# Twelve seven-product steps instead of nine, with one of the three sums on GpSimd and a single ring for the split weights

## The chip, the cores and the metric

One core of a Trainium2 chip runs the whole kernel. The metric is the device time of one execution in microseconds (us). Engines are called TensorE (PE in the profile, PEld for its weight loads), VectorE (DVE), ScalarE (ACT), GpSimd (POOL) and SyncE (SP); SP and POOL issue the DMA transfers.

## The reference

A decoder trunk with `DEPTH = 1`, so only layer 0 and the final norm are computed:

```python
def reference(x, norm_attn, w_in_attn, w_out_attn, ..., final_norm):
    h = x                                     # (1, 256, 4096) float32
    h = h + attn_branch(rms_norm(h, norm_attn), w_in_attn, w_out_attn)
    return rms_norm(h, final_norm)

def attn_branch(xn, w_in, w_out):             # w_in (4096, 16384), w_out (4096, 4096)
    q, k, v, g = jnp.split(xn @ w_in, 4, axis=-1)
    o = stick_breaking_attention(to_heads(q), to_heads(k), to_heads(v))   # 32 heads of 128
    return (o * jax.nn.silu(g)) @ w_out
```

Nearly all the work is the two matrix products, 256 rows of x against 256 MB and 64 MB of float32 weights.

## The kernel before, in words

**Precision.** TensorE multiplies a reduced float32 (fp32r). Each operand is therefore split in two: a high part, a cast on ACT (`wh`), and a low part, the difference on DVE (`wl`, called a low here). One product is three matmuls of 128 x 512: high by high, high by low, low by high (`mm3`).

**Units and steps.** The output is made in units. Units 0 to 15 go over column blocks of the input weights (two column tiles of 512 each: q and k, gate and v), units 16 to 18 over pairs of column blocks of the output weights, and two single units end the kernel. Each unit has 16 steps over the 4096 inner rows; a step takes two weight tiles (`raw`, 128 x 2 x 512, float32), one for each column tile, each with two inner blocks. Seen as a 2 x 2 matrix of blocks by a 2 x 2 matrix of blocks, a step costs eight products in the plain way. In a mixed unit (1 to 15, 17 and 18) the steps of the list `SEVEN` use a Strassen form with seven products, at the price of sums of weight blocks. The other steps have eight products and no sums of weights.

**A seven-step.** The first raw tile is split as it came (part i = 0, two blocks, forms A11 and A12). Of the second tile the second block is split as it came (part 1, form S4). A transfer issued by POOL then adds that second block from memory onto the tile's first block (`add_block`, two DMAs with `accum_op=ALU.add`). Then come three sums of blocks (`sums`), all on DVE: `one[0] -= two[0]`, `two[1] = one[0] + two[1]`, `one[1] += one[0]`. The four summed blocks are split as two parts of two blocks each (i = 2 and 3).

**Rings.** Raw tiles live in 7 places, filled by SP in the order of the steps. The split pairs live in 5 places (`w`), the split single blocks in 2 (`s`). A ring's place is set free when the last product that uses the part is done.

**What sets the order.** The kernel is written as small generators. A planner (`Plan`) runs them in simulated time: each work has an engine, a cost and a key (a due time), and whenever an engine is free in that simulated time the waiting work with the least key is emitted. The result is one fixed instruction order for each engine; the semaphores are put in afterwards. So costs such as `vector_ns`, keys such as `first[c] - SUMS_AHEAD * 1e3` and the order of the list `parts` decide the order, and nothing else of them is left at run time.

Of the kernel before, what the change touches and what calls it, by code (L numbers as in the profile page):

```python
# [11 lines left out]
F32R = mybir.dt.float32r  # L12
BF16 = mybir.dt.bfloat16
AF = mybir.ActivationFunctionType
ALU = mybir.AluOpType
# [4 lines left out]
P = 128  # L20
# [8 lines left out]
W = 2 * CW  # L29
NJ = D // W  # L30
KT = 2
NS = KC // KT
# [6 lines left out]

SEVEN = (1,3,5,7,8,10,11,13,14)
RAW_BUFS = 7
PAIRS = 5
SINGLES = 2
KEPT = PAIRS

SPREAD = (11, 1.1)
HEADS_AHEAD = 3
HEADS_LATER = 12  # L50
AHEAD, SUMS_AHEAD = 4.0, 3.0
PIPE = 0
BLOCKS_LATER = 2


# [7 lines left out]

BOTH, SECOND = slice(0, 2), slice(1, 2)
SEVEN_PARTS = (
    (0, BOTH, ((1, "A11", 0), (2, "A12", 1))),
    (1, SECOND, ((3, "S4", 0),)),
    (1, BOTH, ((7, "S3", 0), (5, "S1", 1))),  # L70
    (0, BOTH, ((6, "S2", 0), (4, "A22", 1))),
)
EIGHT_PARTS = (
    (0, BOTH, ((2, "A11", 0), (2, "A12", 1), (4, "A21", 0), (4, "A22", 1))),
# [12 lines left out]

def scalar_ns(n):
    return 98 + n / 1.2


def tensor_ns(n):
# [138 lines left out]
def kernel(  # L231
# [10 lines left out]
    nc = Plan(tc)  # L242
# [3 lines left out]
    wp = ctx.enter_context(tc.tile_pool(name="weights", bufs=1))  # L246
# [25 lines left out]
    parts, quads = [], []  # L272
    for u, (kind, w, cols) in enumerate(units):
        for s in range(NS):
            if kind == "single":
                if s % 2 == 0:
                    quads.append(((w, cols[0], s), (w, cols[0], s + 1)))
                b = ((1, 6), (7, 2))[u - LAST + 1]
# [10 lines left out]
            for i, (k, place, prods) in enumerate(which):  # L289
                parts.append(  # L290
                    dict(u=u, s=s, i=i, tile=(len(quads) - 1, k), place=place, prods=prods, quad=len(quads) - 1,
                         seven=which is SEVEN_PARTS, size=place.stop - place.start)
                )

    if PIPE:
        late, turn = [], []
        for k, p in enumerate(parts):
            if p["seven"] and p["i"] > 1 and p["s"] < NS - 1:
                late.append(p)
                continue  # L300
            turn.append(p)
            if late and p["s"] != late[0]["s"] and (p["i"] == 1 if p["seven"] else p["i"] == 0):
                now = [q for q in late if q["s"] < p["s"] or q["u"] < p["u"]]
                turn += now
                late = [q for q in late if q not in now]
        assert not late and len(turn) == len(parts)
        parts = turn
# [6 lines left out]
    starts, ends, first, left, place_of = {}, {}, {}, {}, {}  # L314
    PRODUCT = 3 * tensor_ns(W)
    for g, (n, k) in enumerate(order):
        p = parts[n]
        b = p["u"], p["prods"][k][0]
# [19 lines left out]
    def dve(emit, n, key=None, **kw):  # L338
        n = n if isinstance(n, tuple) else (n,)
        cost = sum(vector_ns(m) for m in n) + 122 * (len(n) - 1)  # L340
        return nc.work("vector", cost, emit, soon() if key is None else key, **kw)

    def act(emit, n, key=None, **kw):
        n = n if isinstance(n, tuple) else (n,)
        cost = sum(scalar_ns(m) for m in n) + 100 * (len(n) - 1)
        return nc.work("scalar", cost, emit, soon() if key is None else key, **kw)
# [5 lines left out]
        return nc.work("tensor", 90 + sum(tensor_ns(m) for m in n), emit, nc.here - 1e4, wait=400)  # L352

    def moved(engine, emit, sizes, key, after=None, hold=False, adds=False):
        issue = 550 if engine == "gpsimd" else 330
        return nc.work(
            engine, issue * len(sizes), emit, key, after=after, hold=hold, moves=[(4 * P * n, adds) for n in sizes]
        )

    def together(*works):  # L360
        for w in works:
            nc.start(w)

    for name, places in (
        ("raw", RAW_BUFS), ("w", PAIRS), ("s", SINGLES), ("gh", 3), ("one", 1), ("two", 1),
        ("qkh", 1), ("qkl", 1), ("f", 1), ("att", 1), ("heads", 1),
        *((f"b{b}", 1) for b in range(1, 8)),
    ):
        nc.ring(name, places)


    raw, wh, wl = {}, {}, {}
    lows_left, tile_left = {}, {}
    quad_parts = {}
# [38 lines left out]
    def tile_done(*tile):  # L413
        tile_left[tile] -= 1
        if not tile_left[tile]:
            nc.give("raw")
# [6 lines left out]

    def sums(q):

        a, b, c, d = quad_parts[q]
        one, two = raw[q, 0], raw[q, 1]
        for k in range(2):
            tile_left[q, k] += 1

        def add(to, at_, f, g, key, op=ALU.add):
            return dve(
                lambda: nc.vector.tensor_tensor(out=to[:, :, at_, :], in0=f, in1=g, op=op), W,
                key - SUMS_AHEAD * 1e3,
            )

        yield nc.until(("lows", a), ("T3", q))
        yield add(one, 0, one[:, :, 0, :], two[:, :, 0, :], first[c], ALU.subtract)
        yield nc.until(("lows", b))
        yield add(two, 1, one[:, :, 0, :], two[:, :, 1, :], first[c])  # L440
        nc.tell(("sums", c))
        yield add(one, 1, one[:, :, 0, :], one[:, :, 1, :], first[d])
        nc.tell(("sums", d))
        for k in range(2):
            tile_done(q, k)

    def piece(n, c, there):

# [9 lines left out]
            nc.tell(("low", n, k))  # L458
        low_done(n)

    def split(size, tag, bufs):
        for n, p in enumerate(parts):
            if p["size"] != size:
                continue
            q = p["quad"]
            yield nc.take(tag)
            t = p["tile"][1]
            if q:
                yield nc.until(("raw", q, t))
            wh[n] = wp.tile([P, size, W], F32R, tag=tag + "h", name=f"wh{n}", bufs=bufs)  # L470
            wl[n] = wp.tile([P, size, W], F32R, tag=tag + "l", name=f"wl{n}", bufs=bufs)
            cuts = [slice(k, k + 1) for k in range(KT)] if q == 0 else [slice(0, size)]
            lows_left[n] = len(cuts)
            if p["seven"] and p["i"] == 0:
                nc.start(sums(q))
            for c in cuts:
                if q == 0:
                    there = [("raw", q, t, c.start)]
                else:
                    there = [("sums", n)] if p["seven"] and p["i"] > 1 else [("raw", q, t)]  # L480
                nc.start(piece(n, c, there))


# [105 lines left out]
    for _ in range(WARM):  # L589
# [8 lines left out]
        out=bound, in_=bound, compare_op=ALU.is_gt, fill=0.0, base=0,  # L598
# [23 lines left out]
    def x_stats():  # L622
        for i in range(NT * NQ):
            t, q = divmod(i, NQ)
            w = D // NQ
            yield nc.until(("used", 0, 1 + i * 11 // 16))
            yield nc.take("gh")
            nc.start(x_stat(i, t, q, w))
# [41 lines left out]
    def constants():  # L670
        yield nc.until(("form", "s", 0))
        yield dve(lambda: nc.vector.tensor_copy(neg_tri, tri_f), P)
        nc.give("qkl")
# [293 lines left out]

    def new_h(c):

        if c == NJ - 2:  # L970
            both = wp.tile([P, HG, KT, CW], F32, tag="raw", name=f"h{c}", bufs=RAW_BUFS)
        for t in range(NT):
            if c == NJ - 2:
                hs[c, t] = both[:, t].rearrange("p k n -> p (k n)")
                continue
            pool, tag, bufs = (ep, f"h{c}_{t}", 1)
            if NJ - 4 <= c < NJ - 2:
                pool, tag, bufs = wp, "s" + "hl"[t], SINGLES
            elif c == NJ - 1:
                pool, tag = sp, "x" + "hl"[t] + "0"  # L980
            hs[c, t] = pool.tile([P, W], F32, tag=tag, name=f"h{c}_{t}", bufs=bufs)

# [80 lines left out]
    def mixed_h(u, c):  # L1063
        yield nc.until(("full", u, 1))
        if c + 1 == NJ - 3:
            yield nc.take("s", "s")
        for k in range(2):
            new_h(c + k)
        yield from combine(u, Rows(c), Rows(c + 1), ("C1", "C2"))
        yield nc.until(("C1", u), ("C2", u))  # L1070
        nc.tell(("C", u))
# [61 lines left out]
    def count_down(*name):  # L1133
        left[name] -= 1
        return not left[name]

    def done(n, k):
        p = parts[n]
        u, s = p["u"], p["s"]
        if ends[u, p["prods"][k][0]] == (n, k):  # L1140
            nc.tell(("full", u, p["prods"][k][0]))
        if count_down("part", n):
            nc.give("w" if p["size"] == KT else "s")
        if count_down("step", u, s):
            nc.tell(("used", u, s))

# [12 lines left out]
    def products():  # L1159
        for g, (n, k) in enumerate(order):  # L1160
            p = parts[n]
            u, s = p["u"], p["s"]
            b, f, c = p["prods"][k]
            if u < 1:
                what = "s"
            elif u < OUT0:
                what = "n"
            elif u == OUT0:
                what = "o"
            else:  # L1170
                what = "r" if u > LAST - 2 and s in SEVEN else "p"
            if starts[u, b] == (n, k):
                yield nc.take(f"b{b}")
                ev.setdefault(u, {})[b] = acc.tile([P, W], F32, tag=f"b{b}", name=f"acc{u}_{b}")
            yield nc.until(("low", n, c), ("form", what, s), lead=nc.LEAD)
            yield nc.work(
                "tensor", PRODUCT, lambda: product(n, k), g * PRODUCT, after=lambda n=n, k=k: done(n, k), hold=False
            )
            nc.here = g * PRODUCT

    together(split(KT, "w", PAIRS), split(1, "s", SINGLES), products(), x_stats(), x_factor(), constants())

    def in_turn(works):
        for w in works:
# [54 lines left out]
```

## Time and profile before

| | |
|---|---|
| median of 3 runs | 1756.4 us (1754.83 to 1757.13) |
| profiled execution, its span | 1754.0 us |
| busy in that span: PE, PEld, DVE, ACT, POOL | 1736.9, 1427.1, 1560.4, 1166.4, 295.7 us |
| mean granted TensorE clock | 0.997 |
| bytes moved by DMA | 405.86 MB, mean 231 GB/s |

The page gives no other time of the profiled execution than its span, so the span stands for it. A busy time is the union of an engine's instructions; all helpers record under one line (L115), so groups are told apart by tile names: `wh` casts, `wl` lows, `raw` sums and loads, `acc` products, `f`, `a`, `z`, `o` the heads' work between units.

### The profile page before, as it was taken

What the parts mean: (1) busy time and instruction counts of PE and PEld (TensorE: products, weight loads), DVE (VectorE), ACT (ScalarE), POOL (GpSimd) and SP (SyncE); (2) the same over time, 40 slices, a digit from 0 to 9 for tenths busy, and PEclk for the clock granted to TensorE, in tenths of its full rate; (3) what the DMA queues carried; (4) which work ended last, traced back from release to release, by engine and by line L of the source; (5) the groups of instructions that cost most, each with busy time, mean ns of one, the idle gap of its engine ahead of it and who ended that gap; (6) DMA issues with size and microseconds to landing.
All of it is one profiled execution on the core that took longest, in us unless ns stands there. A gap on an engine that the chain in (4) does not pass through costs nothing.

```text
span 1754.0 us, 24699 instructions
## 1 busy us (share of the span) xinstructions
PE 1736.9 (99%) x7806; PEld 1427.1 (81%) x7806; DVE 1560.4 (89%) x1971; ACT 1166.4 (67%) x1594; POOL 295.7 (17%) x364
## 2 busy tenths in 40 slices
PE   8999999999999999999999999999999999999997
PEld 6888888888888888888888888888888888888885
DVE  7889999999999999999999999999999997899963
ACT  7975767676767676767676767676767675666543
POOL 0012121111111121211111111111112111111100
PEclk9999999999999999999999999999999999999998
DMA  9968777777777878787878787878786877889874
GB/s 340 316 192 224 230 218 229 223 223 226 222 228 217 239 210 239 208 245 210 240 208 245 208 239 206 242 202 245 200 246 200 262 244 239 229 245 271 257 236 156
DMA packets 242867, 405.86 MB, mean 231 GB/s; under 512 B 27520, under 2 KB 67968, under 8 KB 242736
## 3 DMA queue, kind: packets, MB, share of 16 engines
q1 hardware_dynamic: 193968, 352.15, 60.8%
q0 software_dynamic: 47184, 49.76, 17.3%
q10 hardware_dynamic: 1584, 2.38, 0.4%
q8 instruction: 61, 1.00, 0.2%
q14 instruction: 70, 0.57, 0.1%
HBM read 396.05 MB, written 8.13 MB: 230 GB/s over the span
## 4 chain that ended last, share of the span: by engine, by line
PE 92%; DVE 3%; issue 2%; DMA 2%; ACT 1%; SPq 0%; ACTq 0%; DVEq 0%
PE acc L115 87%; PE z L115 2%; DVE wl L115 2%; PE o L115 2%; DMA raw<-in_w_in_dram 1%; PE tr L115 1%; ACT wh L115 1%; DVE raw L115 0%; ACT h L115 0%; SPq L115 0%; DMA xres<-in_x_dram 0%; DMA raw<-in_w_out_dram 0%; ACTq L115 0%; DVE gv_sb L115 0%; DVE h L115 0%
## 5 line engine op out<-in xcount | busy, mean ns | idle before, releaser
L115 ACT CAST wh<-raw 128x1024 fp32r<-128x1024 f32 (+1 forms) x948 | 886.1, 976 | 476.1 <-issue 173.3
L115 DVE TENSOR_TENSOR wl<-raw,wh 128x1024 fp32r<-128x1024 f32 (+1 forms) x948 | 1032.1, 1131 | 125.3 <-ACT wh L115 118.6
L115 PE MATMUL acc<-wh,sh 128*128 128x512 f32 x1913 | 762.6, 399 | 2.4 <-DVE sh L115 2.1
L115 PE MATMUL acc<-wh,sl 128*128 128x512 f32 x1913 | 746.2, 390 | 0.0
L115 PE MATMUL acc<-wl,sh 128*128 128x512 f32 x1913 | 744.9, 389 | 0.8 <-DVE wl L115 0.8
L115 PEld LDWEIGHTS acc<-wh,sh 128*128 128x128 f32 x1913 | 359.4, 188 | 77.3 <-DVE gv_sb L115 3.9
L115 PEld LDWEIGHTS acc<-wh,sl 128*128 128x128 f32 x1913 | 359.1, 188 | 76.9 <-DVE sl L115 0.8
L115 PEld LDWEIGHTS acc<-wl,sh 128*128 128x128 f32 x1913 | 359.7, 188 | 71.5 <-DVE wl L115 1.5
L115 POOL DMA_DIRECT2D raw<-in_w_in_dram x270 | 236.1, 987 | 1075.7 <-DMA raw<-in_w_in_dram 403.1
L115 DVE TENSOR_TENSOR raw<-raw,raw 128x512 f32<-128x512 f32 x306 | 210.3, 687 | 5.1
L115 PE MATMUL acc<-wh,oh 128*128 128x512 f32 x494 | 193.2, 391 | 0.0
L115 PE MATMUL acc<-wl,oh 128*128 128x512 f32 x494 | 192.4, 389 | 0.6 <-DVE wl L115 0.6
L115 PE MATMUL acc<-wh,ol 128*128 128x512 f32 x494 | 192.3, 389 | 0.0
L115 PEld LDWEIGHTS acc<-wl,oh 128*128 128x128 f32 x494 | 92.8, 188 | 20.5 <-DVE wl L115 1.2
L115 PEld LDWEIGHTS acc<-wh,oh 128*128 128x128 f32 x494 | 92.8, 188 | 19.3 <-DVE gv_sb L115 0.4
L115 PEld LDWEIGHTS acc<-wh,ol 128*128 128x128 f32 x494 | 92.7, 188 | 19.2
L115 DVE TENSOR_TENSOR raw<-raw 128x512 f32<-128x512 f32 x153 | 104.5, 683 | 0.0
L115 POOL DMA_DIRECT2D raw<-in_w_out_dram x36 | 31.6, 992 | 132.5 <-DMA raw<-in_w_out_dram 66.2
L115 ACT ACTIVATE f<-f 128x384 f32<-128x384 f32 x96 | 50.5, 526 | 3.0
L115 DVE SCALAR_TENSOR_TENSOR f<-z,f 128x384 f32<-128x384 f32 x32 | 17.8, 557 | 31.2 <-ACT f L115 31.2
L115 POOL DMA_DIRECT2D p<-spill x33 | 20.3, 696 | 129.6 <-DVE ol L115 94.0
L115 ACT ACTIVATE gl<-gl 128x512 f32<-128x512 f32 x48 | 30.0, 625 | 7.3 <-DVE gl L115 7.3
(90 smaller groups left out, 745.9 us busy)
## 6 DMA issues: line engine op xcount, KB each, us to landing
raw<-in_w_in_dram SPq DMA_DIRECT2D x1020, 256.0 KB, 4.6
raw<-in_w_out_dram SPq DMA_DIRECT2D x256, 256.0 KB, 3.9
raw<-in_w_in_dram POOLq DMA_DIRECT2D x270, 128.0 KB, 5.2
raw<-in_w_out_dram POOLq DMA_DIRECT2D x36, 128.0 KB, 5.6
xr<-in_x_dram SPq DMA_DIRECT2D x16, 256.0 KB, 5.2
xres<-in_x_dram SPq DMA_DIRECT2D x16, 256.0 KB, 5.6
xs<-in_xT_dram SPq DMA_DIRECT2D x15, 256.0 KB, 5.3
spill<-gated POOLq DMA_DIRECT2D x15, 256.0 KB, 3.9
```

The lines of the kernel that those rows point to most:

```text
L115: return self.tc.keep_in_program_order(getattr(self.engine, name)(*args, **kw))
```

## The change

1. `SEVEN` has twelve steps instead of nine.
2. The third sum is an add on GpSimd, started after the first sum and due 25 us (`POOL_AHEAD`) ahead of its product in the planner's terms. The planner's cost for a GpSimd transfer rises from 550 to 950 ns.
3. The four summed blocks are four parts of one block each (i = 2 to 5). For steps below 14 the last two (i = 4 and 5) stand behind the first two parts of the next step in the list `parts`.
4. All split blocks share one tile of twelve places, freed block by block; a pair takes two neighbouring places, with a skip at the ring's end.
5. Near the end, the output tiles that lay in the ring `s` lie in two more places of the raw ring.

```diff
-SEVEN = (1,3,5,7,8,10,11,13,14)
+SEVEN = (1, 2, 3, 5, 6, 7, 9, 10, 11, 12, 13, 14)
 RAW_BUFS = 7
-PAIRS = 5
-SINGLES = 2
-KEPT = PAIRS
+SLOTS = 12
+KEPT = 5
-PIPE = 0
+PIPE = 1
+LATE_UNTIL = 14
+LATE_FROM = 4
+POOL_AHEAD = 2.5e4
 SEVEN_PARTS = (
     (0, BOTH, ((1, "A11", 0), (2, "A12", 1))),
     (1, SECOND, ((3, "S4", 0),)),
-    (1, BOTH, ((7, "S3", 0), (5, "S1", 1))),
-    (0, BOTH, ((6, "S2", 0), (4, "A22", 1))),
+    (1, FIRST, ((7, "S3", 0),)),
+    (0, FIRST, ((6, "S2", 0),)),
+    (1, SECOND, ((5, "S1", 0),)),
+    (0, SECOND, ((4, "A22", 0),)),
 )
+def pool_ns(n):
+    return 400 + 2.9 * n
...
-            if p["seven"] and p["i"] > 1 and p["s"] < NS - 1:
+            if p["seven"] and p["i"] >= LATE_FROM and p["s"] < LATE_UNTIL:
...
-        issue = 550 if engine == "gpsimd" else 330
+        issue = 950 if engine == "gpsimd" else 330
...
+        def last():
+            yield pool_add(one[:, :, 1, :], one[:, :, 0, :], one[:, :, 1, :], first[e] - POOL_AHEAD)
+            nc.tell(("sums", e))
+            tile_done(q, 0)
+
         yield nc.until(("lows", a), ("T3", q))
         yield add(one, 0, one[:, :, 0, :], two[:, :, 0, :], first[c], ALU.subtract)
+        nc.tell(("sums", c))
+        nc.start(last())
         yield nc.until(("lows", b))
-        yield add(two, 1, one[:, :, 0, :], two[:, :, 1, :], first[c])
-        nc.tell(("sums", c))
-        yield add(one, 1, one[:, :, 0, :], one[:, :, 1, :], first[d])
+        yield add(two, 1, one[:, :, 0, :], two[:, :, 1, :], first[d])
         nc.tell(("sums", d))
...
+    hi_ring = wp.tile([P, SLOTS, W], F32R, name="wh")
+    lo_ring = wp.tile([P, SLOTS, W], F32R, name="wl")
...
-            yield nc.take(tag)
+            if at_ + size > SLOTS:
+                extra = SLOTS - at_
+                at_ = 0
+            yield nc.take(*["w"] * (size + extra))
...
-        if c == NJ - 2:
+        if NJ - 4 <= c < NJ - 1:
             both = wp.tile([P, HG, KT, CW], F32, tag="raw", name=f"h{c}", bufs=RAW_BUFS)
...
-        if count_down("part", n):
-            nc.give("w" if p["size"] == KT else "s")
+        place_uses[n, c] -= 1
+        if not place_uses[n, c]:
+            nc.give(*["w"] * slots_of[n][c])
```

How the order changes on DVE, in the middle of a mixed unit of the attention part. Before, one seven-step: `raw_0_7118` is its first raw tile, `raw_1_7071` its second.

```order
L115 TENSOR_TENSOR wl_7202<-raw_0_7118,wh_7201 128x1024
L115 TENSOR_TENSOR raw_0_7118<-raw_0_7118,raw_1_7071 128x2x256
L115 TENSOR_TENSOR raw_1_7071<-raw_0_7118,raw_1_7071 128x2x256
L115 TENSOR_TENSOR raw_0_7118<-raw_0_7118 128x2x256
L115 TENSOR_TENSOR wl_7225<-raw_1_7071,wh_7224 128x1024
L115 TENSOR_TENSOR wl_7235<-raw_0_7118,wh_7234 128x1024
L115 TENSOR_TENSOR wl_7252<-raw_0_7131,wh_7251 128x1024
```

Now, in such a unit: `raw_0_6791` and `raw_1_6783` are the two tiles of one seven-step, 6776 and 6751 those of the step before, 6855 and 6802 those of the step after. The low of its own first pair stands a few rows ahead of this piece.

```order
L123 TENSOR_TENSOR raw_0_6791<-raw_0_6791,raw_1_6783 128x2x256
L123 TENSOR_TENSOR wl<-raw_1_6751,wh 128x512
L123 TENSOR_TENSOR wl<-raw_0_6776,wh 128x512
L123 TENSOR_TENSOR wl<-raw_0_6855,wh 128x1024
L123 TENSOR_TENSOR wl<-raw_1_6802,wh 128x512
L123 TENSOR_TENSOR wl<-raw_1_6783,wh 128x512
L123 TENSOR_TENSOR raw_1_6783<-raw_0_6791,raw_1_6783 128x2x256
L123 TENSOR_TENSOR wl<-raw_0_6791,wh 128x512
L123 TENSOR_TENSOR raw_0_6855<-raw_0_6855,raw_1_6802 128x2x256
L123 TENSOR_TENSOR wl<-raw_1_6783,wh 128x512
L123 TENSOR_TENSOR wl<-raw_0_6791,wh 128x512
```

The three sums in a row have become two that stand apart, with the lows of the neighbouring steps between; the lows of pairs of summed blocks are single ones, and the last two of a step stand behind the next step's first sum.

On POOL, in the attention part. Before, only transfers (the added blocks, and one spill of a unit's gated heads):

```order
L115 DMA raw_1_8577<-in_w_in_dram 128x256 x2
L115 DMA spill_8688<-gated_8506 128x512
L115 DMA raw_1_8673<-in_w_in_dram 128x256 x2
L115 DMA raw_1_8746<-in_w_in_dram 128x256 x2
L115 DMA raw_1_8817<-in_w_in_dram 128x256 x2
```

Now:

```order
L123 DMA raw_1_8403<-in_w_in_dram 128x256 x2
L123 TENSOR_TENSOR raw_0_8395<-raw_0_8395 128x2x256
L123 DMA raw_1_8454<-in_w_in_dram 128x256 x2
L123 TENSOR_TENSOR raw_0_8446<-raw_0_8446 128x2x256
L123 TENSOR_TENSOR raw_0_8493<-raw_0_8493 128x2x256
L123 DMA raw_1_8582<-in_w_in_dram 128x256 x2
```

An add stands between most pairs of transfers, so a transfer can be queued behind an add and an add behind a transfer. On TensorE the list of matmul rows is 153 shorter (7561 to 7408), which is 51 products of three.

More of the change, by code (lines that the diff above doesn't have):

```diff
@@ L62 @@
 PLACES = {f: k for forms in (SEVEN_FORMS, EIGHT_FORMS) for k, f in enumerate(forms)}
-BOTH, SECOND = slice(0, 2), slice(1, 2)
+BOTH, FIRST, SECOND = slice(0, 2), slice(0, 1), slice(1, 2)
 SEVEN_PARTS = (
@@ L341, in dve, with pool_add @@
         return nc.work("vector", cost, emit, soon() if key is None else key, **kw)
+    def pool_add(to, f, g, key, op=ALU.add):
+        return nc.work(
+            "gpsimd", pool_ns(W), lambda: nc.gpsimd.tensor_tensor(out=to, in0=f, in1=g, op=op), key
+        )
     def act(emit, n, key=None, **kw):
@@ L364 @@
     for name, places in (
-        ("raw", RAW_BUFS), ("w", PAIRS), ("s", SINGLES), ("gh", 3), ("one", 1), ("two", 1),
+        ("raw", RAW_BUFS), ("w", SLOTS), ("gh", 3), ("one", 1), ("two", 1),
         ("qkh", 1), ("qkl", 1), ("f", 1), ("att", 1), ("heads", 1),
@@ L424, in sums @@
     def sums(q):
-        a, b, c, d = quad_parts[q]
+        a, b, third, c, d, e = quad_parts[q]
         one, two = raw[q, 0], raw[q, 1]
@@ L435, in add @@
             )
+        def last():
+            yield pool_add(one[:, :, 1, :], one[:, :, 0, :], one[:, :, 1, :], first[e] - POOL_AHEAD)
+            nc.tell(("sums", e))
+            tile_done(q, 0)
         yield nc.until(("lows", a), ("T3", q))
         yield add(one, 0, one[:, :, 0, :], two[:, :, 0, :], first[c], ALU.subtract)
+        nc.tell(("sums", c))
+        nc.start(last())
         yield nc.until(("lows", b))
-        yield add(two, 1, one[:, :, 0, :], two[:, :, 1, :], first[c])
-        nc.tell(("sums", c))
-        yield add(one, 1, one[:, :, 0, :], one[:, :, 1, :], first[d])
+        yield add(two, 1, one[:, :, 0, :], two[:, :, 1, :], first[d])
         nc.tell(("sums", d))
-        for k in range(2):
-            tile_done(q, k)
+        tile_done(q, 1)
     def piece(n, c, there):
@@ L459, in piece, with split @@
         low_done(n)
-    def split(size, tag, bufs):
-        for n, p in enumerate(parts):
-            if p["size"] != size:
-                continue
-            q = p["quad"]
-            yield nc.take(tag)
+    hi_ring = wp.tile([P, SLOTS, W], F32R, name="wh")
+    lo_ring = wp.tile([P, SLOTS, W], F32R, name="wl")
+    place_uses, slots_of = {}, {}
+    for n, p in enumerate(parts):
+        for _, _, c in p["prods"]:
+            place_uses[n, c] = place_uses.get((n, c), 0) + 1
+    def split():
+        at_ = 0
+        for n, p in enumerate(parts):
+            size, q = p["size"], p["quad"]
+            extra = 0
+            if at_ + size > SLOTS:
+                extra = SLOTS - at_
+                at_ = 0
+            yield nc.take(*["w"] * (size + extra))
+            slots_of[n] = [1] * size
+            slots_of[n][0] += extra
             t = p["tile"][1]
@@ L469, in split @@
                 yield nc.until(("raw", q, t))
-            wh[n] = wp.tile([P, size, W], F32R, tag=tag + "h", name=f"wh{n}", bufs=bufs)
-            wl[n] = wp.tile([P, size, W], F32R, tag=tag + "l", name=f"wl{n}", bufs=bufs)
+            wh[n] = hi_ring[:, at_ : at_ + size, :]
+            wl[n] = lo_ring[:, at_ : at_ + size, :]
+            at_ += size
             cuts = [slice(k, k + 1) for k in range(KT)] if q == 0 else [slice(0, size)]
@@ L479, in split @@
                 else:
-                    there = [("sums", n)] if p["seven"] and p["i"] > 1 else [("raw", q, t)]
+                    there = [("raw", q, t)]
+                    if p["seven"] and p["i"] > 1:
+                        there = [("T3", q) if p["i"] == 2 else ("sums", n)]
                 nc.start(piece(n, c, there))
@@ L968, in new_h @@
     def new_h(c):
-        if c == NJ - 2:
+        if NJ - 4 <= c < NJ - 1:
             both = wp.tile([P, HG, KT, CW], F32, tag="raw", name=f"h{c}", bufs=RAW_BUFS)
         for t in range(NT):
-            if c == NJ - 2:
+            if NJ - 4 <= c < NJ - 1:
                 hs[c, t] = both[:, t].rearrange("p k n -> p (k n)")
@@ L976, in new_h @@
             pool, tag, bufs = (ep, f"h{c}_{t}", 1)
-            if NJ - 4 <= c < NJ - 2:
-                pool, tag, bufs = wp, "s" + "hl"[t], SINGLES
-            elif c == NJ - 1:
+            if c == NJ - 1:
                 pool, tag = sp, "x" + "hl"[t] + "0"
@@ L1065, in mixed_h @@
         if c + 1 == NJ - 3:
-            yield nc.take("s", "s")
+            yield nc.take("raw", "raw")
         for k in range(2):
@@ L1141, in done @@
             nc.tell(("full", u, p["prods"][k][0]))
-        if count_down("part", n):
-            nc.give("w" if p["size"] == KT else "s")
+        c = p["prods"][k][2]
+        place_uses[n, c] -= 1
+        if not place_uses[n, c]:
+            nc.give(*["w"] * slots_of[n][c])
         if count_down("step", u, s):
@@ L1179, in products @@
             nc.here = g * PRODUCT
-    together(split(KT, "w", PAIRS), split(1, "s", SINGLES), products(), x_stats(), x_factor(), constants())
+    together(split(), products(), x_stats(), x_factor(), constants())
     def in_turn(works):
```

## The prediction

> **What bounds the kernel now.** I read the page's busy times first, then the chain that ended last, then the chain in order of time, then a table of stretches.
>
> ```profile
> span 1754.0 us, 24699 instructions
> PE 1736.9 (99%) x7806; PEld 1427.1 (81%) x7806; DVE 1560.4 (89%) x1971; ACT 1166.4 (67%) x1594; POOL 295.7 (17%) x364
> PE 92%; DVE 3%; issue 2%; DMA 2%; ACT 1%; SPq 0%; ACTq 0%; DVEq 0%
> 222.85 48.33 PE acc L115 x213
> 396.56 48.31 PE acc L115 x213
> 1440.66 157.10 PE acc L115 x693
> 560.00:650.00 90.00, 90.00 (x410) 74.10 (x409) 82.53 (x100) 61.98 (x83) 16.29 (x19) 1.00 0.80 225
> 650.00:740.00 90.00, 90.00 (x409) 74.16 (x408) 82.89 (x101) 59.87 (x80) 16.33 (x19) 1.00 0.78 228
> ```
>
> TensorE makes 92% of the chain. The columns of the stretches are length, busy PE, PEld, DVE, ACT, POOL, then granted clock, DMA share and GB/s: in the middle PE is busy 90.00 of 90.00 us at clock 1.00. A piece of the chain that recurs, 48.3 us of 213 matmuls, starts at 222.85 and again at 396.56: two units of the program in 173.71 us, so **86.86 us a unit**. 693 matmuls in 157.10 us are 0.2267 us each, so a product of three matmuls takes **0.680 us**. DVE stands close behind: (82.53 + 82.89) / 180 = 91.9% of the time, 79.8 us of each unit. ACT (60.9 of 90) and POOL (16.3 of 90) are far off.
>
> The span of the profiled execution is 1754.0 us, 2.4 below the median of the runs, 1756.4; I make the sum as a difference and put it on the median. Runs lie within 1754.83 to 1757.13, so about 0.2% (3.5 us) is what a measurement can tell from no change.
>
> **What goes from TensorE.** A step of a mixed unit with eight products becomes one with seven in three more of the sixteen steps. There are 15 mixed units on the input weights and 2 on the output weights: 17 x 3 = 51 products, 51 x 0.680 = **34.7 us** off the engine that sets the end. If all else kept up, a unit would take 86.86 - 2.04 = 84.82 us and the kernel 1756.4 - 34.7 = **1721.7 us**. This is the floor of the range.
>
> **What comes to DVE.** Rates first. DVE instructions overlap at their ends, so the interval from start to start counts.
>
> ```profile
> 757.62 3.50 DVE L115 TENSOR_TENSOR wl<-raw,wh 128x1024 fp32r<-128x1024 f32 x3 [0.64 <-ACT wh L115]
> 785.82 0.68 DVE L115 TENSOR_TENSOR gv_sb<-acc,gv_sb 128x512 f32<-128x512 f32 x1
> 786.42 1.21 DVE L115 TENSOR_TENSOR wl<-raw,wh 128x1024 fp32r<-128x1024 f32 x1
> 787.55 0.68 DVE L115 TENSOR_TENSOR gv_sb<-acc,gv_sb 128x512 f32<-128x512 f32 x1
> ```
>
> An add of 512 columns lets the next one start after 0.60 us (785.82 to 786.42), one of 1024 after 1.13 us (786.42 to 787.55), each 0.08 us before its own end. A seven-step had three lows of 1024, one of 512 and three sums: 3 x 1.13 + 4 x 0.60 = 5.79 us. Now it has one low of 1024, five of 512 and two sums: 1.13 + 7 x 0.60 = 5.33. So the cut into single blocks costs 4 x 0.60 - 2 x 1.13 = 0.14 and the sum that leaves saves 0.60. An eight-step keeps two lows, 2.26. Per unit: 9 x 5.79 + 7 x 2.26 = 67.9 before, 12 x 5.33 + 4 x 2.26 = 73.0 after, **+5.1 us**. On 79.8 that is 84.9 us of DVE in a unit that TensorE could do in 84.82. The busy time counts 0.08 us too much at each idle stretch:
>
> ```profile
> DVE wl L115 <- ACT wh L115: 118.6, 182, 3.5
> DVE f L115 <- ACT f L115: 31.2, 30, 1.4
> ACT wh L115 <- PE acc L115: 135.7, 105, 3.7
> POOL raw L115 <- DMA raw<-in_w_in_dram: 403.1, 66, 10.4
> ```
>
> Some 212 such stretches over 20 units, 11 a unit, are 0.9 us, so DVE needs **84.0 us** back to back. Its cover is gone: it may lose 0.8 us a unit before TensorE starves, and 2.9 us before the gain is spent. Of its waits now (149.8 us in these two rows, 7.5 a unit), those on ACT's casts come since sum, cast and low stand next to each other; the new order puts other lows between, so I take most of them at nothing. What ACT gains, three short casts for each new seven-step and the cut pairs, is cheap beside its 30% of idle time.
>
> **What comes to GpSimd.** 204 adds (12 x 17) and 102 more adding transfers (3 x 17 x 2).
>
> ```profile
> 0.42 0.10 POOL L1226 MEMSET const-uint8-127<- 128x1 uint8 x1
> 1.09 0.29 POOL masks.py:199 TENSOR_SCALAR_AFFINE_SELECT ident<-ident 128x128 f32<-128x128 f32 x1
> L115 POOL DMA_DIRECT2D raw<-in_w_in_dram x270 | 236.1, 987 | 1075.7 <-DMA raw<-in_w_in_dram 403.1 <-DVE raw L115 226.3 <-DVE wl L115 210.2
> L115 DVE TENSOR_TENSOR wl<-raw,wh 128x1024 fp32r<-128x1024 f32 x791 | 935.7, 1220 | 120.2 <-ACT wh L115 113.5 <-DMA raw<-in_w_in_dram 2.2 <-DMA xres<-in_x_dram 1.5
> ```
>
> The trace has no GpSimd add. Nearest is the select of 128 columns, 0.29 us, against 0.10 for one column: 0.19 / 127 = 1.5 ns a column and input. For 512 columns that gives 0.10 + 0.77 = 0.87 us if both inputs come at once, 1.64 if one after the other. With two transfers at 0.99 each a seven-step takes 2.9 to 3.6 us of POOL, 12 of them 34 to 43 of 85 us: POOL itself has room.
>
> A new wait: the cast and low of the late block wait for the add, and behind them, in order, all later casts and lows. From the first sum to that low stand ten DVE instructions, 6.5 us; a pair of transfers ahead, the add and the cast are 1.98 + 1.64 + 0.6 = 4.2 at most. It is hidden unless POOL sits at a transfer whose tile has not landed (403 us in 66 waits above, harmless so far, as nothing stood behind them).
>
> The open cost is c, what such an add takes from DVE while it reads the same memory. No row shows a GpSimd instruction that reads tiles beside DVE work; the select ran before DVE had any. Bounds: 0 (the POOL transfers above lie all through the span, and the DVE lows beside them keep a mean of 1220 ns, the 1.21 us seen above), and 1.64 (DVE stands for the whole add). Three facts choose: DVE is busy 84 of 85 us; 73.0 of those are lows and sums, each reading two tensors from the memory that the add reads; and c need only reach 2.9 / 12 = **0.24 us** to make the kernel slower. Six sevenths of the interval lie beyond. I take the select's price: 0.77 us of reading, met by a DVE add 73.0 / 84.0 of the time, 0.67, and 0.08 of overlap lost at the restart, c = **0.75**.
>
> The Trainium skill (SBUF — State Buffer, Who interferes with whom) says that a Vector instruction with two SBUF inputs contends with a GpSimd instruction that reads SBUF, and that the one that starts first keeps the shared pair for its whole instruction. No run here shows it so far. Its GPSIMD Engine Reference (Performance versus the Vector engine) measures 4497 ns for a two-input add of 2048 columns; by that my estimate for 512 is 1.1 to 1.2 us, and the sum, were DVE to stand for all of it, would end near 1940.
>
> **Sum.** 84.0 + 12 x 0.75 = 93.0 us a unit, DVE-bound, +6.1 on 86.86; x 17 = +104. The waits for loads of the second rival fall away then, since a slower DVE gives loads more time. 1756.4 + 104 = **1860 us**. With c half way down to its lower bound (0.4) and half way up to its upper (1.2): 88.8 to 98.4 us a unit, 1789 to 1952.
>
> **Moves in the rings.** A raw tile is now held from its first low to the low of the late block. Counting DVE's instructions in the new order at the rates above, the first tile of a seven-step is held 1.13 + 12 x 0.60 + 1.13 = 9.5 us where it was 3 x 1.13 + 3 x 0.60 = 5.2.
>
> ```profile
> raw<-in_w_in_dram SPq DMA_DIRECT2D x1020, 256.0 KB, 4.6
> raw<-in_w_in_dram POOLq DMA_DIRECT2D x270, 128.0 KB, 5.2
> SPq L115 <- DVE wl L115: 976.2, 527, 8.7
> L115 ACT CAST wh<-raw 128x1024 fp32r<-128x1024 f32 x791 | 803.1, 1048 | 459.9 <-issue 173.3 <-PE acc L115 128.8 <-DVE raw L115 94.2
> q1 hardware_dynamic: 193968, 352.15, 60.8%
> q0 software_dynamic: 47184, 49.76, 17.3%
> ```
>
> SP issues a load when a DVE low has set a tile free (976 us of waiting), so this loop is live. Seven places turn in 3.5 steps, 3.5 x 84.82 / 16 = 18.6 us. The first tile needs 4.6 to land, 1.05 for the cast, and 9.5: 15.2, room enough. The second needs 4.6 + 2 x 0.99 + 5.2 = 11.8 to its added block, then ten DVE instructions, 6.5, to its last low: 18.3 of 18.6, and now POOL's add may stand ahead of its transfers (0.87 to 1.64), with the adding queue at 17.3 x 408 / 306 = 23%. On the average of both tiles it fits, tile by tile hardly. The one ring of twelve places holds what 5 pairs and 2 singles held; freed block by block it gives ACT its room earlier (135.7 us of waits on PE now), cost nothing. Three more h tiles in raw places near the end leave four for the last units: two loads ahead, 10.9 us of products against 4.6 + 1.05 + 1.13, nothing.
>
> **The rivals.**
>
> *TensorE still bounds (0.33).* c is under 0.2 and the loads arrive. For it: POOL's transfers leave DVE's rate alone, and the new order puts one or two lows between each sum and what needs it. Against it: DVE has 0.8 us in 85. At 84.8 to 86.5 a unit: 1722 to 1750, the likeliest 1735.
>
> *DVE waits for its tiles (0.21).* c is small, but the 0.3 us of spare time in the second tile's loop is taken by an add ahead on POOL. The full 0.87 in half of the 12 steps is 5 us; less 0.3 spare each, about 3.5. From 0.8 a unit on TensorE starves, from 2.9 on it is slower: 84.0 + 3.5 = 87.5, +0.6 x 17 = 1767; 1752 to 1790. This is the slower case that needs nothing from the memory.
>
> *A small c that just eats the gain (0.04).* With c = 0.24 the unit is 86.9 us again and the time 1756. That TensorE's work does not shrink at all is no rival: the new program has 153 matmul rows fewer.
>
> **How the numbers follow.** Forecast 0.42 (DVE held by GpSimd, 1860), rivals 0.33, 0.21, 0.04. Faster by over 0.2%: 0.33. Within: 0.04, the last rival. Slower: 0.42 + 0.21 = 0.63. Cases of both signs: the forecast's own range is 1789 to 1952. For 8 in 10 the range must take in the faster rival but for its last few microseconds: low 1724 (0.06 below), high 1950 (0.1 above).
>
> **What would show it.** Right: DVE lows of 512 columns, 0.68 us now, have a mean clearly over 0.75 us and DVE is busy 97% or more in the stretches; PE is no longer busy 90 of 90 and waits for wl; the unit is near 93 us; the GpSimd add is longer than 0.87 us. Wrong by the first rival: lows stay at 0.68, a unit takes 85 us with PE at 90 of 90. By the second: lows stay at 0.68, but DVE waits for adding transfers, for GpSimd's add or for ACT casts that wait for a load, and the unit is 87 to 88 us.

## The result

The changed kernel takes 2014.7 us (median of 4 runs, 2013.7 to 2017.3) against 1756.8 for the kernel before on the same chip, a ratio of 1.147 (95% interval 1.1455 to 1.1487). Forecast were 1860 us and a range that ended at 1950: the side was right, the size was not. Over 17 mixed units the 258 us are 15.2 a unit, 102 us where it was 86.86.

From the page of the changed kernel, its busy times, and from its stretches (columns as before: length, busy PE, PEld, DVE, ACT, POOL, granted clock, DMA share, GB/s):

```profile
span 2015.3 us, 26649 instructions
PE 1818.9 (90%) x7653; PEld 1426.1 (71%) x7653; DVE 1782.4 (88%) x2460; ACT 1299.7 (64%) x2113; POOL 981.2 (49%) x676
560.00:650.00 90.00, 79.09 (x328) 60.09 (x326) 80.81 (x111) 58.55 (x96) 51.82 (x32) 0.96 0.74 199
650.00:740.00 90.00, 81.46 (x340) 64.72 (x341) 82.29 (x107) 58.12 (x95) 46.58 (x32) 0.94 0.70 197
```

TensorE has its 153 matmuls fewer, but waits a tenth of the time, and its granted clock is 0.94 to 0.96 there, where it was 1.00. Whether that lower clock adds to the time is not shown apart. DVE is not busier than before: it too waits. The groups by shape (count, busy us, mean ns, idle before and its releasers) and the waits say for what:

```profile
L123 POOL TENSOR_TENSOR raw<-raw 128x512 f32<-128x512 f32 x204 | 611.9, 3000 | 496.4 <-ACT wh L123 171.2 <-issue 103.3 <-DVE raw L123 84.5
L123 DVE TENSOR_TENSOR wl<-raw,wh 128x512 fp32r<-128x512 f32 x1024 | 743.5, 756 | 112.9 <-ACT wh L123 112.2
L123 DVE TENSOR_TENSOR wl<-raw,wh 128x1024 fp32r<-128x1024 f32 x434 | 553.8, 1290 | 49.9 <-ACT wh L123 48.5 <-DMA raw<-in_w_in_dram 0.8
L123 DVE TENSOR_TENSOR raw<-raw,raw 128x512 f32<-128x512 f32 x408 | 306.7, 752 | 1.9 <-DMA raw<-in_w_in_dram 1.1 <-DMA raw<-in_w_out_dram 0.5
ACT wh L123 <- POOL raw L123: 229.9, 87, 5.1
DVE wl L123 <- ACT wh L123: 160.7, 117, 3.4
PEld acc L123 <- DVE wl L123: 156.1, 167, 2.9
PE acc L123 <- DVE wl L123: 89.8, 117, 2.6
```

Before, DVE's lows of 512 columns and its sums of two tiles were shorter:

```profile
L115 DVE TENSOR_TENSOR wl<-raw,wh 128x512 fp32r<-128x512 f32 x157 | 107.2, 683 | 5.1 <-ACT wh L115 5.1
L115 DVE TENSOR_TENSOR raw<-raw,raw 128x512 f32<-128x512 f32 x306 | 210.3, 687 | 5.1
```

The GpSimd add lasts 3.00 us in the mean. DVE's instructions have grown from 683, 1220 and 687 ns: 1024 x 73 + 434 x 70 + 408 x 65 ns = 132 us. ACT waits 230 us for the add, and DVE's lows 161 us for casts. TensorE's matmuls wait 90 us for lows and its weight loads 156 us; the two overlap, and TensorE is idle for 196 us of the span in all. The timeline shows both directions. One add held a low of 1024 columns, which took 1.94 us in place of 1.22:

```profile
704.27 1.29 POOL L123 TENSOR_TENSOR raw<-raw 128x512 f32<-128x512 f32 x1 [2.22 <-DMA raw<-in_w_in_dram]
704.71 1.94 DVE L123 TENSOR_TENSOR wl<-raw,wh 128x1024 fp32r<-128x1024 f32 x1
```

Fifteen microseconds later DVE kept an add out:

```profile
719.26 0.68 DVE L123 TENSOR_TENSOR wl<-raw,wh 128x512 fp32r<-128x512 f32 x1
719.86 0.55 DVE L123 TENSOR_TENSOR fl<-f,fh 128x384 fp32r<-128x384 f32 x1
720.33 1.88 DVE L123 TENSOR_TENSOR wl<-raw,wh 128x512 fp32r<-128x512 f32 x3
722.14 0.68 DVE L123 TENSOR_TENSOR raw<-raw,raw 128x512 f32<-128x512 f32 x1
722.74 1.22 DVE L123 TENSOR_TENSOR wl<-raw,wh 128x1024 fp32r<-128x1024 f32 x1
726.70 0.42 DVE L123 TENSOR_TENSOR a<-a,bound 128x256 f32<-128x256 f32 x1 [2.75 <-ACT a L123]
719.48 5.59 POOL L123 TENSOR_TENSOR raw<-raw 128x512 f32<-128x512 f32 x1 [2.42 <-ACT fh L123]
725.11 0.62 ACT L123 CAST wh<-raw 128x512 fp32r<-128x512 f32 x1 [4.16 <-POOL raw L123]
725.63 0.48 ACT L123 ACTIVATE a<-z 128x384 f32<-128x384 f32 x1
```

DVE runs without a gap until 723.96 (722.74 + 1.22). The add, started at 719.48, ends at 725.07, 1.11 us after DVE stopped. ACT stood 4.16 us at the cast that needs it, with the heads' work (`a`) queued behind, and so DVE in turn stood 2.75 us. This is no single case: 198 of the 204 adds stand in a row of their own in the timeline, 56 of these last over 3.5 us, and each of the 56 ends 1.11 to 1.16 us after DVE has run out of work. DVE's gaps at these 56 places come to 124 us.

### The profile page after: what moved, and what is told of

It reads as the page before. It is cut to its first block, busy times and chain, and to the rows that moved or that the text cites. A ratio compares the mean times of both kernels' runs of the same rounds, so it can differ in the third digit from the quotient of the medians.

```text
span 2015.3 us, 26649 instructions
## 1 busy us (share of the span) xinstructions
PE 1818.9 (90%) x7653; PEld 1426.1 (71%) x7653; DVE 1782.4 (88%) x2460; ACT 1299.7 (64%) x2113; POOL 981.2 (49%) x676
## 5 line engine op out<-in xcount | busy, mean ns | idle before, releaser
L123 DVE TENSOR_TENSOR wl<-raw,wh 128x512 fp32r<-128x512 f32 (+1 forms) x1458 | 1273.3, 915 | 162.7 <-ACT wh L123 160.7
L123 ACT CAST wh<-raw 128x512 fp32r<-128x512 f32 (+1 forms) x1458 | 1016.5, 745 | 596.9 <-POOL raw L123 229.9
L123 POOL TENSOR_TENSOR raw<-raw 128x512 f32<-128x512 f32 x204 | 611.9, 3000 | 496.4 <-ACT wh L123 171.2
L123 PE MATMUL acc<-wl,sh 128*128 128x512 f32 x1868 | 759.1, 406 | 68.7 <-DVE wl L123 67.2
L123 POOL DMA_DIRECT2D raw<-in_w_in_dram x360 | 322.6, 1039 | 307.8 <-DMA raw<-in_w_in_dram 77.3
L123 DVE TENSOR_TENSOR raw<-raw,raw 128x512 f32<-128x512 f32 x408 | 306.7, 752 | 1.9 <-DMA raw<-in_w_in_dram 1.1
L123 PE MATMUL o<-a,gv_sb 128*128 128x128 f32 (+1 forms) x128 | 33.6, 394 | 41.0 <-ACT gated L123 40.8
L123 PEld LDWEIGHTS o<-a,gv_sb 128*128 128x128 f32 x128 | 26.1, 217 | 52.6 <-ACT gated L123 48.0
L123 POOL DMA_DIRECT2D raw<-in_w_out_dram x48 | 43.1, 1110 | 26.1 <-DMA raw<-in_w_out_dram 15.5
```

The source lines that it names most:

```text
L123: return self.tc.keep_in_program_order(getattr(self.engine, name)(*args, **kw))
```

## The experiments

**Theory H**: a GpSimd add and a DVE instruction with two inputs in the tile memory exclude each other; either the add waits, and what waits for it, or DVE is held. **Rival R**: the rings, the late order and the loads of twelve steps cost the time. **Rival P**: a GpSimd instruction costs by its place in POOL's queue, ahead of the adding transfers.

### Parts of the change by themselves

**Third sum on DVE, the rest as changed.**

```diff
-            yield pool_add(one[:, :, 1, :], one[:, :, 0, :], one[:, :, 1, :], first[e] - POOL_AHEAD)
+            yield add(one, 1, one[:, :, 0, :], one[:, :, 1, :], first[e])
```

> The changed kernel with its third sum back on DVE; twelve seven-steps, single blocks, late order and one ring stay. Theory H (a GpSimd add and a DVE instruction with two inputs in SBUF exclude each other; the add waits for a gap, DVE or ACT then waits for it): no DVE instruction is longer than its 0.68 or 1.22 us any more, DVE has 84.0 + 12 x 0.60 = 91.2 us a unit and is busy all the time, so 1757 + 17 x (91.2 - 86.86) = about 1830 us. Rival R (rings, late order and loads of twelve steps cost the time, GpSimd little): near the changed kernel's 2015, at least above 1950, since loads and DVE get no easier.

Measured 1849.4 us, ratio 1.053 (1.0514 to 1.0546). By shape, and in a stretch:

```profile
L123 DVE TENSOR_TENSOR wl<-raw,wh 128x512 fp32r<-128x512 f32 x1024 | 667.6, 683 | 6.6 <-ACT wh L123 6.6
L123 DVE TENSOR_TENSOR wl<-raw,wh 128x1024 fp32r<-128x1024 f32 x434 | 523.9, 1218 | 54.0 <-ACT wh L123 51.8 <-DMA raw<-in_w_out_dram 1.3
560.00:650.00 90.00, 85.88 (x381) 68.14 (x380) 89.03 (x134) 65.64 (x106) 21.53 (x25) 1.00 0.83 225
```

The same instructions have their old lengths, 683 and 1218 ns, and DVE is busy 98.9%. There is more DVE work, and 165 us less time than with the sum on GpSimd. That speaks against R. The kernel is now bound by DVE's own load: (1849.4 - 1756.2) / 17 = 5.5 us over 86.86, 92.3 a unit where the load counted gave 91.2.

**No third sum at all.** This kernel leaves the sum out, so its output is another; only its time is used.

```diff
-            yield pool_add(one[:, :, 1, :], one[:, :, 0, :], one[:, :, 1, :], first[e] - POOL_AHEAD)
+            yield nc.until(("sums", c))
```

> The changed kernel without the third sum (left out: the late block is split as it was loaded), all else as it is. Theory H: neither DVE nor GpSimd does it, DVE has 84.0 us a unit, TensorE 84.8; 1722 to 1765 us, the later the more the loads of the raw ring are late. Rival R: 1850 us or more.

Measured 1753.2 us, ratio 0.9984 (0.9972 to 0.9995); DVE in a stretch of it is busy 97.6%.

```profile
650.00:740.00 90.00, 88.82 (x405) 72.76 (x404) 87.85 (x131) 69.08 (x113) 22.16 (x26) 1.00 0.85 235
PE 1712.7 (98%) x7653; PEld 1396.8 (80%) x7653; DVE 1627.0 (93%) x2460; ACT 1297.1 (74%) x2113; POOL 388.4 (22%) x472
DVE wl L123 <- ACT wh L123: 56.8, 67, 3.4
```

So the rest of the change, with twelve steps, is worth -3.0 us (1753.2 against 1756.2 in these runs), and the GpSimd add by itself costs 2014.7 - 1753.2 = 261 us, 1.28 for each of 204. DVE's own time shows how this cost is made up: over the profiled spans, 2015.3 and 1750.8 us, DVE is busy 1782.4 against 1627.0 us, 155 more with the same instructions, and idle 233 against 124, 109 more. Of the 109, 104 are lows that wait for casts (160.7 against 56.8). But 31 us are missing to the floor of 1721.7.

**Third sum on GpSimd, nothing else.** The kernel before, nine steps, pairs and two rings, with the add of the changed kernel in `sums`.

```diff
-        yield add(one, 1, one[:, :, 0, :], one[:, :, 1, :], first[d])
+        def last():
+            yield pool_add(one[:, :, 1, :], one[:, :, 0, :], one[:, :, 1, :], first[d] - 2.5e4)
+            ...
+        nc.start(last())
```

> The kernel before with its third sum on GpSimd and nothing else changed (nine seven-steps, pairs, two rings). Theory H: 153 adds cost DVE 0.65 us each (100 us) and save it 0.60 each (92 us), DVE has 10% of idle time, but each pair behind the add waits for it: slower than before, 1790 to 1870 us. Rival R: the add takes work off DVE and harms nothing, 1757 us, no change.

Measured 1794.1 us, ratio 1.0217 (1.0201 to 1.0234): slower, though DVE lost 92 us of work and in a stretch is busy only 75.5 of 90 us.

```profile
560.00:650.00 90.00, 88.29 (x397) 71.31 (x395) 75.46 (x88) 58.24 (x78) 34.13 (x28) 1.00 0.77 222
DVE wl L119 <- ACT wh L119: 216.1, 207, 3.5
ACT wh L119 <- POOL raw L119: 31.6, 16, 2.7
```

DVE waits 216 us for casts where it was 119. ACT stands only 32 us for the add itself; how much of the rest the add causes is not shown apart. Relief of an engine that was not the bound bought nothing, and the net loss is 38 us.

**Nine steps, sum on DVE, the rest as changed.** The edit of the first experiment and `SEVEN` of before.

> The changed kernel with its third sum on DVE and the nine seven-steps of before: only single blocks, late order and the one ring are left of the change. Theory H: DVE has 79.8 + 9 x 0.14 = 81 us, TensorE 86.9: no change, 1753 to 1761 us. Rival R: rings and late order cost time by themselves, 1800 us or more.

Measured 1750.4 us, ratio 0.9966 (0.9954 to 0.9979). Single blocks, late order and one ring do no harm; they even win 6 us, a little more than I had allowed for. Rival R is out as the cause of the slower time.

### What a GpSimd instruction does to DVE

The next three are the kernel before, all three sums on DVE, with one extra GpSimd work for each of the 153 seven-steps, between spare tiles, for whose result nothing waits.

```diff
+            yield nc.work("gpsimd", 1900, emit, first[d] - 2.5e4)
     # emit, in turn:
+    nc.gpsimd.tensor_tensor(out=spare[:, 512:1024], in0=spare[:, 0:512], in1=spare[:, 0:512], op=ALU.add)
+    for _ in range(3): nc.gpsimd.memset(spare[:, 512:1024], 0.0)
+    nc.gpsimd.tensor_copy(spare[:, 512:1024], spare[:, 0:512])
```

> The kernel before with all three sums on DVE and, beside each seven-step's sums, one more GpSimd add of 512 columns between spare tiles (153 in all), for whose result nothing waits. Theory H: the adds last 1.3 to 5 us, as they wait for DVE, and some 30 or more DVE instructions with two inputs are longer by 1.06 us; DVE's idle 10% takes most of it, so 1760 to 1800 us. Rival P (a GpSimd instruction costs only by its place in POOL's queue ahead of transfers): no DVE instruction is longer, and the time is that of the kernel with fills.

> The same with three GpSimd fills of 512 columns in place of each spare add: they write and read nothing. Theory H: no DVE instruction is longer than 0.68 or 1.22 us, 1753 to 1762 us. Rival P: as slow as with spare adds.

> The kernel before with a GpSimd copy of 512 columns between spare tiles for each seven-step: one input read instead of two. If any reading by GpSimd holds a DVE instruction with two inputs: some DVE instructions longer by 0.5 to 0.7 us, 1800 to 1870 us. If only two-input adds do: none longer, 1757 us.

Measured: adds 1935.7 us, 1.1022 (1.1004 to 1.1041), far above what I expected; fills 1757.8, 1.0005 (0.9995 to 1.0014), no change; copies 1846.5, 1.0509 (1.0488 to 1.053). The groups by shape of the adds (with DVE's busy time), of the fills and of the copies, in this order:

```profile
PE 1803.2 (93%) x7806; PEld 1431.3 (74%) x7806; DVE 1751.7 (90%) x1971; ACT 1164.7 (60%) x1594; POOL 483.0 (25%) x518
L115 POOL TENSOR_TENSOR spare<-spare 128x512 f32<-128x512 f32 x153 | 252.6, 1651 | 1.4
L115 DVE TENSOR_TENSOR wl<-raw,wh 128x1024 fp32r<-128x1024 f32 x791 | 1037.8, 1353 | 106.8 <-ACT wh L115 106.4 <-PE z L115 0.2
L115 DVE TENSOR_TENSOR raw<-raw,raw 128x512 f32<-128x512 f32 x306 | 255.7, 836 | 5.6
```

```profile
L115 POOL MEMSET spare<- 128x512 f32 x459 | 314.9, 686 | 18.5
L115 DVE TENSOR_TENSOR wl<-raw,wh 128x1024 fp32r<-128x1024 f32 x791 | 933.8, 1221 | 119.5 <-ACT wh L115 119.0
L115 DVE TENSOR_TENSOR raw<-raw,raw 128x512 f32<-128x512 f32 x306 | 210.6, 688 | 5.6
```

```profile
L115 POOL COPY spare<-spare 128x512 f32<-128x512 f32 x153 | 224.9, 1470 | 0.9
L115 DVE TENSOR_TENSOR wl<-raw,wh 128x1024 fp32r<-128x1024 f32 x791 | 983.8, 1284 | 102.3 <-ACT wh L115 98.3 <-DMA xs<-in_xT_dram 1.5 <-DMA raw<-in_w_out_dram 0.7
L115 DVE TENSOR_TENSOR raw<-raw,raw 128x512 f32<-128x512 f32 x306 | 232.1, 759 | 5.6
```

The fills keep POOL longer (315 us) than the adds do (253) and the lows stay at 1221 ns: rival P is out, on this kernel the queue is not it. Adds lengthen the lows to 1353 and the sums to 836 ns: in these two groups 791 x 133 + 306 x 149 ns = 151 us of the 179 lost. The copies, with one input, lose 89 us: 791 x 64 + 306 x 72 ns = 73 of them in these groups. So it is GpSimd's reading that DVE is held by, about twice as long for two inputs as for one, even when it reads tiles that DVE never touches. My price for the spare adds was wrong since I let DVE's 10% of idle time take it; nearly all came out at the end. With the spare adds DVE is idle for 187 us of its span (1939.1 - 1751.7) where it was 194 (1754.0 - 1560.4): that idle time is mostly waits, sum then cast then low, not room.

**Held only, on the changed kernel.** No third sum, as above, but 204 spare adds in its place, for which nothing waits; eleven ring places make room for the spare tiles.

> The changed kernel without the third sum (left out), but with 204 GpSimd adds of 512 columns between spare tiles at its place in the order, for which nothing waits; eleven ring places instead of twelve, to make room for the spare tiles. It parts the two ways in which the add can cost: DVE held, and casts waiting for a late add. Theory H1 (being held is all, 1.17 us an add as with the spare adds on the kernel before): 1753 + 204 x 1.17 = about 1990 us, near the changed kernel. Theory H2 (half is the wait for the late add): 1753 + 135 us of longer DVE instructions = about 1890 us.

Measured 1991.9 us (two runs, 1983 and 2001), ratio 1.1337 (1.1277 to 1.1397). The number is H1's 1990, but DVE's times are not H1's:

```profile
PE 1802.7 (90%) x7653; PEld 1427.3 (71%) x7653; DVE 1819.8 (91%) x2460; ACT 1303.1 (65%) x2113; POOL 1008.7 (50%) x677
L123 POOL TENSOR_TENSOR spare<-spare 128x512 f32<-128x512 f32 x204 | 728.1, 3569 | 2.4
L123 DVE TENSOR_TENSOR wl<-raw,wh 128x512 fp32r<-128x512 f32 x1024 | 749.5, 763 | 6.8 <-ACT wh L123 6.5
L123 DVE TENSOR_TENSOR wl<-raw,wh 128x1024 fp32r<-128x1024 f32 x434 | 581.3, 1351 | 52.4 <-ACT wh L123 49.3 <-DMA raw<-in_w_in_dram 1.9 <-DMA raw<-in_w_out_dram 0.7
L123 DVE TENSOR_TENSOR raw<-raw,raw 128x512 f32<-128x512 f32 x408 | 327.1, 802 | 84.7 <-DMA raw<-in_w_in_dram 72.4 <-DMA raw<-in_w_out_dram 11.9
```

In these groups DVE is held 1024 x 80 + 434 x 131 + 408 x 115 ns = 186 us, more than the changed kernel's 132, and its sums wait 84 us for adding transfers, which stand behind the adds in POOL's order (3.57 us in the mean), where the changed kernel shows 1.6. Against the kernel without the sum, DVE is busy 193 us more (1819.8 against 1627.0) and idle 55 more (1999.0 - 1819.8 = 179 against 124). So the same exclusion costs both kernels some 240 to 260 us and is split otherwise: where nobody waits for the add, 193 us of held time and 55 of waits; where a cast waits for it, 155 and 109. That the totals come so near each other is not explained, and since 55 us of it are waits, which H1 put at nothing, H1 met its number in part by luck.

### Other ways to the same sum

**Ten steps, sum on DVE.** `SEVEN = (1, 3, 5, 6, 8, 9, 10, 12, 13, 14)`.

> The changed kernel's single blocks, late order and one ring with the third sum on DVE and ten seven-steps. DVE has 84.0 - 2 x 3.07 + 10 x 0.60 = 83.9 us a unit, TensorE 86.86 - 0.68 = 86.2. Theory H with the loads' waits as seen without the third sum: 1739 to 1752 us, under both kernels. Rival R: DVE at 97% waits for loads, 1757 to 1775 us.

Measured 1749.7 us, ratio 0.996 (0.9948 to 0.9973): as fast as nine steps, with TensorE short of full by 0.1 us in the 90 shown:

```profile
560.00:650.00 90.00, 89.90 (x410) 74.26 (x409) 87.39 (x126) 65.95 (x102) 18.95 (x22) 1.00 0.80 229
```

**The sum as an adding transfer from tile to tile, eleven steps.**

```diff
-            yield pool_add(one[:, :, 1, :], one[:, :, 0, :], one[:, :, 1, :], first[e] - POOL_AHEAD)
+            yield moved("gpsimd", lambda: nc.gpsimd.dma_start(one[:, :, 1, :], one[:, :, 0, :], accum_op=ALU.add), ...)
```

> The changed kernel with the third sum as an adding transfer from tile to tile, issued by POOL, and eleven seven-steps: neither DVE nor GpSimd's own cores add. DVE has 84.0 - 3.07 = 80.9 us a unit, TensorE 85.5. Theory H: no DVE instruction is longer; if the transfers keep up 1733 to 1745 us. Rival L (transfer engines, at 85% already without the third sum at twelve steps, and the 5 us until it lands): late blocks wait for the transfer, 1757 to 1800 us.

Measured 1915.9 us, ratio 1.0907 (1.0887 to 1.0927). No DVE instruction is longer, but:

```profile
560.00:650.00 90.00, 83.76 (x362) 65.92 (x360) 76.83 (x110) 62.48 (x99) 32.42 (x33) 0.98 0.92 238
q0 software_dynamic: 108000, 108.11, 35.7%
ACT wh L123 <- DMA raw<-raw: 101.5, 60, 4.2
```

The transfer engines are busy 92%, the adding queue takes 35.7% of them, and casts wait 101.5 us for the summed blocks to land: rival L, and beyond its 1800.

**One more raw place, one less in the ring.** `RAW_BUFS = 8`, `SLOTS = 11`, on the kernel without the third sum and on the one with ten steps.

> The changed kernel without the third sum (left out), with eight raw places and eleven ring places. Twelve places gave 1753 against TensorE's floor of 1722. If late loads are those 31 us: 1725 to 1742 us. If DVE's 84 of 85 us and its dependences are: 1748 to 1757 us.

> The kernel with the sum on DVE and ten seven-steps, with eight raw places and eleven ring places in place of seven and twelve. If waits for loads hold it above TensorE's 1745 us: 1744 to 1748 us. If the split ring is what is short: 1750 us or more.

Measured 1735.9 us, ratio 0.988 (0.986 to 0.99), and 1743.8, ratio 0.9923 (0.9906 to 0.9939). Without the third sum, the waits of ACT for loads on the input weights were 88.8 us with seven raw places and are 17.4 with eight:

```profile
ACT wh L123 <- DMA raw<-in_w_in_dram: 88.8, 64, 3.7
ACT wh L123 <- DMA raw<-in_w_in_dram: 17.4, 15, 2.1
```

So one more raw place is worth 17 of the missing 31 us, and with it the waits for late loads went; the other 14 I leave to DVE's load and its dependences, not shown apart. Ten steps with the sum on DVE and eight raw places is faster than both kernels of this case, and TensorE is full again:

```profile
560.00:650.00 90.00, 90.00 (x412) 74.83 (x411) 87.71 (x128) 67.09 (x104) 19.96 (x24) 1.00 0.80 230
```

## Why the prediction was right and wrong

**TensorE's 34.7 us** were right as work, 153 matmuls fewer, and reached only in part: 1735.9, without the third sum, is the nearest that a run came to 1721.7.

**DVE's +5.1 us a unit** was right: with the sum left out DVE is busy 97.6% of the stretch shown, with it back on DVE 98.9%. Nine steps without the GpSimd add show that single blocks and late order cost nothing.

**The mechanism** was the forecast's in one half: DVE lows of 512 columns rose over 0.75 us (to 0.756), and the GpSimd add held DVE. The sign "DVE busy 97% or more" did not come (81 and 82 of 90 us), since DVE itself waited for casts.

**The step that failed is the new wait, costed at nothing.** c, what an add takes from DVE, was right in size: DVE is busy 155 us more for 204 adds, 0.76 an add where I took 0.75. Part of that is luck. I built it on an add of 0.87 us, while the shortest in the changed kernel last 1.28, and where nothing waited for the add on the kernel before, 153 adds cost 1.17 us each. The forecast was 155 us short of 2014.7, and of that some 109 are DVE's new idle time, 104 of them lows that wait for casts, while ACT's casts wait 230 us for adds. I had counted what the add takes from DVE and not what DVE takes from the add: I bounded its length by 1.64 us and called the late block's wait hidden behind ten DVE instructions, 6.5 us, "4.2 at most". The add lasts 3.00 us in the mean and 5.59 in the row above, with two transfers, a cast and the queue of ACT behind it: the work that was to cover the add kept it out, until DVE ran dry. The two terms are also not free of each other, since an add that does not wait holds DVE instead. One row of the run with spare adds on the kernel before:

```profile
627.71 1.37 POOL L115 TENSOR_TENSOR spare<-spare 128x512 f32<-128x512 f32 x1
627.63 2.55 DVE L115 TENSOR_TENSOR wl<-raw,wh 128x1024 fp32r<-128x1024 f32 x1 [0.51 <-ACT wh L115]
```

The low took 2.55 us in place of 1.22, beside an add of 1.37. The remaining 45 us were missing without any add: my sum starts from 84.0 us a unit of DVE, 1756.4 - 17 x 2.86 = 1708 us, and the kernel without the third sum takes 1753. I had let TensorE's floor (14 us of these) and the waits for loads fall away.

The Trainium skill (SBUF — State Buffer, Who interferes with whom) agrees with the runs in that two-input DVE instructions are held by GpSimd's reads and not by its fills. Its rule that the one that starts first keeps the memory for its whole instruction fits the add at 704.27, but not the row just shown, where the low is recorded as starting 0.08 us before the add and is held all the same. By the figure of the Trainium skill's GPSIMD Engine Reference (Performance versus the Vector engine) I had put the sum near 1940, closer than by the select; the wait of the late block was in neither.

**The rivals.** That TensorE still bounds, at 0.33, was much too high: even with no add at all the kernel stays at 1753. The second rival, late loads, was real beside the add: without the third sum one more raw place won 17 us.

## What to carry to other kernels

Giving an elementwise work to GpSimd did not take it off a full DVE whose own work reads two tiles: each add of 512 columns cost 1.28 us in the changed kernel, and 1.17 beside the kernel before, to save 0.60. To price such a move, put the work beside the old kernel on spare tiles first: adds, copies and fills, side by side, tell what is held and by what. Then ask what waits for the moved work, since work that waits for a pause of DVE stops its own followers. And the idle share of an engine in a chain of dependent works need not be room: DVE's 10% of idle time took up nearly nothing of the held time here.

## What was not expected of the hardware

DVE can keep a GpSimd add out over many instructions, not only for the one that runs: an add of 5.59 us beside a row of DVE instructions without a gap, and adds of 3.57 us in the mean where nothing waited for them. A GpSimd copy, one input, holds DVE too: 89 us for 153 of them. What lets an add in between two DVE instructions in one place and not in another stays open.
